# Low halves of the first stage's weights: an accumulating transfer in place of VectorE's subtraction

## The chip, the cores and the metric

The kernel runs on one core of a Trainium2 chip. The metric is the device time of one execution in microseconds, 2017.48 us as the median of three runs of the kernel before (2017.06 to 2017.93). The core has TensorE (PE in the profile, with its weight loads as PEld), VectorE (DVE), ScalarE (ACT), GpSimd (POOL) and SyncE (SP), which issues most of the transfers; each works through a queue of its own in order, and they wait for one another by semaphores. SP's and POOL's transfers run on the core's 16 DMA engines.

## The reference

One layer of an encoder on 16 learned and 1024 given tokens of width 1024, all in float32:

```python
h = rmsnorm(h_res, norm1_w[l])
proj = h @ w_in[l]                       # 1024 x 9248
(q, k, v, z, b_raw, a_raw, sc_b, sc_c, sc_x, gate_a, gate_b) = jnp.split(proj, SPLIT_POINTS, axis=-1)
o_dn = gated_deltanet_bidir(q, k, v, z, b_raw, a_raw, ...)
y_a = o_dn @ w_branch_dn[l]
y_b = (sc_b * depthwise_conv_centred(sc_c * sc_x, sc_conv_w[l])) @ w_branch_sc[l]
merged = jax.nn.sigmoid(gate_a) * y_a + jax.nn.sigmoid(gate_b) * y_b
h_res = h_res + merged @ w_out[l]
gu = rmsnorm(h_res, norm2_w[l]) @ w_gate_up[l]
h_res = h_res + (jax.nn.silu(gu[..., :D_FF]) * gu[..., D_FF:]) @ w_down[l]
```

`gated_deltanet_bidir` runs a short convolution over q, k and v, normalises q and k by head, and does a chunked delta-rule scan forwards and backwards for each of 8 heads of 128 columns. The output is a last RMSNorm without the 16 learned tokens.

## The kernel before

**Products in three parts.** A float32 operand is held as two float32r halves: a high half (a rounded copy) and a low half (what the copy lost). A product is high by high, high by low and low by high, so a weight tile of 128 columns needs `wh` and `wl`, each [128, 8, 128]: 128 partitions, 8 blocks of 128 rows of the weight matrix, 128 columns. A matmul holds one block of `wh` or `wl` stationary and moves a part of `hTh` (high half of the input) or `al` (its low half) past it.

**The first stage** takes about half of the kernel. Its work is cut into 69 units of 128 columns of `w_in`: 24 for q, k and v, 24 for the short convolution's three inputs, 16 gates and 5 of z. A unit has two or three column ranges of tokens, and for each 8 steps of three matmuls (line 321), in the order high-high, high-low, low-high; so the third matmul of a unit's first step needs `wl`. Between the steps the kernel puts the small matmuls of the delta rule's other work, which runs head by head: decays, norms, an inverse of triangular blocks, and the scan (lines 787 to 865), where PE, DVE and ACT hand each other small tiles. The order of everything in this stage is written out by a planner at build time. It keeps a clock for each engine (`T`), adds an estimate for each instruction (`V(n)` for DVE, `A(n)` for ACT, `pe(ns)`), and takes up a piece of the head's work at the step where its clocks say that the inputs are there.

**Weights of a unit.** At the start of unit n, `pick` has SP load the raw weights of unit n+2 (line 917, 512 KB into one of two `raw` slots), and `wtiles` takes the tiles `wh` and `wl` for unit n+1 (two buffers each). `split_part` then makes the halves of unit n+1 in four parts of four blocks each, at the steps given by `SPL`, here 11 to 14 of unit n: ACT copies to `wh` (line 927), DVE writes `wl` as raw minus `wh` (line 924), twice in turn. The first two units' low halves are made by POOL at the start (line 1052), and the third's before the loop by `split_part`.

**POOL** has little else: clearing of row buffers (370, 371, 410), of `small`, `fP`, `mP`, `XT`, a small product (555), and for each head a chain of 30 tiny operations (646, 648) on a 16 x 16 block.

**Later stages** load their weights with the same column blocks of 128 (`wload` for the branches, `stationary1` for the feed-forward part), always through SP, and split them with ACT and DVE (lines 86 and 87).

Of the kernel before, what the change touches and what calls it, by code (L numbers as in the profile page):

```python
# [16 lines left out]
P = 128  # L17
# [16 lines left out]
    0, 1024, 2048, 3072, 4096, 4128, 5152, 6176, 7200, 8224)  # L34


@with_exitstack
def encoder_layer(ctx: ExitStack, tc: tile.TileContext, x, meta, norm1_w, w_in,
                  dn_conv_w, A_log, dt_bias, dn_norm_w, sc_conv_w, w_bdn, w_bsc,
                  w_out, norm2_w, w_gu, w_down, final_w, out):  # L40
    nc = tc.nc
    x, out = x[0], out[0]
    w_in, w_bdn, w_bsc, w_out, w_gu, w_down = (
        w_in[0], w_bdn[0], w_bsc[0], w_out[0], w_gu[0], w_down[0])

    keep = ctx.enter_context(tc.tile_pool(name="keep", bufs=1))
    keep.tile([P, 24], F32, name="pad")
# [37 lines left out]
    def split(hi, lo, src):  # L85
        nc.scalar.copy(hi, src)  # L86
        nc.vector.tensor_tensor(out=lo, in0=src, in1=hi.bitcast(F32), op=ALU.subtract)  # L87
# [11 lines left out]
    def staged(shape):  # L99
        return *wtiles(shape), rawtile(shape)  # L100

    def wload(src, c0, n=P):
        wh, wl, raw = staged([P, KT, P])
        nc.sync.dma_start(raw[:, :, :n], src[:, c0:c0 + n].rearrange("(k p) c -> p k c", p=P))
        split(wh[:, :, :n], wl[:, :, :n], raw[:, :, :n])
        return wh, wl

    def wrows(src, r0):
# [798 lines left out]
    def pick():  # L907

        mid = fill_units and fill_units[0][3] in (1, 2)
        if qkv_units and not mid and qkv_ok():  # L910
            u = qkv_units.pop(0)
        elif fill_units:
            u = fill_units.pop(0)
        else:
            return None
        raw = rawtile([P, KT, P])
        nc.sync.dma_start(raw, w_in[:, u[0]:u[0] + P].rearrange("(k p) c -> p k c", p=P))
        return [u, None, raw, [0]]

    def split_part(u, i):  # L920
        u[3][0] = i + 1
# [48 lines left out]
    with tc.tile_pool(name="st", bufs=1) as st:  # L970
# [18 lines left out]
        for t, xr in enumerate(xs):  # L989
            if t == 0:  # L990
                nc.sync.dma_start(xr[:META], meta)
                nc.sync.dma_start(xr[META:P], x[0:P - META])
                nc.sync.dma_start(w1one, norm1_w[0:1, :])
            else:
                nc.sync.dma_start(xr[:size(t)], x[P * t - META:P * t - META + size(t)])
            if t == 2:
                units.append(pick())

                nc.sync.dma_start(rows[:120, 0], dn_conv_w[0].rearrange("k (t p) -> (k t) p", p=P))
                nc.sync.dma_start(rows[:24, 1], sc_conv_w[0].rearrange("k (t p) -> (k t) p", p=P))  # L1000
                nc.sync.dma_start(rows[24:25, 1], dn_norm_w)
                nc.sync.dma_start(raw, w_in[:, OBA:OBA + 32].rearrange("(k p) c -> p k c", p=P))
            elif t == 5:
                units.append(pick())
        u0, u1 = units
# [296 lines left out]
                yield T["act"]  # L1302

    dn = ph1.enter_context(tc.tile_pool(name="dn", bufs=1))
    SPL = (11, 12, 13, 14)
    for g in (gen0, gen1):
        for _ in g:
            pass
# [1 line left out]
    while done < H or qkv_units or fill_units or any(ahead):  # L1310
        u = ahead.pop(0)
        if u is None:
            run_streams()
            pump()
            T["pe"] += 100
            ahead.append(pick())
            continue
        for k in range(u[3][0], 4):
            split_part(u, k)
        if ahead[0]:  # L1320
            ahead[0][1] = wtiles([P, KT, P])
        ahead.append(pick())
        for n_, _ in enumerate(u[0][1](u[1])):
            if ahead[0] and n_ in SPL:
                split_part(ahead[0], SPL.index(n_))
            run_streams()
            pump()
    ph1.close()
# [14 lines left out]
    mg = [big("mA", [P, 4, SEQ], F32), big("mB", [P, 4, SEQ], F32)]  # L1343
    szs = {}
    for h in range(ZH, H):
        w = wload(w_in, OZ + h * P)
        sz = szs[h] = mg[1][:, h - ZH]
        for i in range(2):
            po = psany()
            dense(po, w, hx, C0 + META + 512 * i, 512)  # L1350
            sl = slice(512 * i, 512 * i + 512)
            nc.scalar.activation(sz[:, sl], po, AF.Tanh, scale=0.5)
            nc.vector.scalar_tensor_tensor(out=sz[:, sl], in0=sz[:, sl], scalar=1.0, in1=po, op0=ALU.add, op1=ALU.mult)
# [19 lines left out]

    gated_order = [*range(ZH, H), *range(ZH)]
    for j in range(KT):
        w = wload(w_bsc, j * P)
        if j == 0:
            for h in range(ZH, H):
                gated(gated_order.pop(0))
# [8 lines left out]
            gated(gated_order.pop(0))  # L1388
    woh, wol = four("w")
    for j in range(KT):  # L1390
        w = wload(w_bdn, j * P)
        ta = s4(SEQ)
        nc.sync.dma_start(ta, ta_d[j])
        for i in range(2):
# [63 lines left out]
    def stationary1(j):  # L1458

        gh, gl = wtiles([P, KT, P])  # L1460
        rg = rawtile([P, KT, P])
        spare.extend(rawtile([P, KT, P]) for _ in range(0 if j else 2))
        ru = rawtile([P, KT, P])
        nc.sync.dma_start(rg, w_gu[:, j * P:j * P + P].rearrange("(k p) c -> p k c", p=P))
        nc.sync.dma_start(ru, w_gu[:, FF + j * P:FF + j * P + P].rearrange("(k p) c -> p k c", p=P))
        if j:
            split(gh, gl, rg)
        return rg, ru, {"A11": (gh[:, 0:4], gl[:, 0:4]), "A12": (gh[:, 4:8], gl[:, 4:8])}, (gh, gl)
# [234 lines left out]
    for n, (a, b, bank) in enumerate((("A11", "B11", bank_x), ("A12", "B21", bank_y), ("S2", "T2", bank_x), ("S1", "T1", bank_y),  # L1703
# [30 lines left out]
                finish(4 + t)  # L1734


_INS = ["x", "meta_tokens", "norm1_w", "w_in", "dn_conv_w", "A_log", "dt_bias", "dn_norm_w", "sc_conv_w",
        "w_branch_dn", "w_branch_sc", "w_out", "norm2_w", "w_gate_up", "w_down", "final_norm_w"]


# [17 lines left out]
```

## Time and profile before

| | |
|---|---|
| median of three runs | 2017.48 us |
| the profiled execution | 2017.61 us |
| its span, first to last instruction | 2015.9 us |
| PE busy | 1994.2 us (99%) |
| DVE busy | 1359.8 us (67%) |
| ACT busy | 819.4 us (41%) |
| POOL busy | 119.6 us (6%) |
| share of PE in the chain that ended last | 88% |

The first stage lasts from the start to about 1045 us of the span. Busy time of PE counts a matmul from its start to its modelled end; since matmuls overlap, 99% doesn't mean that each starts as soon as it could. A wait is given as `engine tile line <- engine tile line`: who sat idle, and whose end released it. In a timeline the columns are start, duration, engine, line, operation, output and inputs, count, and in brackets the idle time before it with what ended it.

### The profile page before, as it was taken

The page shows a single profiled execution, that of the slowest core. Times are in us where ns is not written, and L with a number is a line of the kernel's source. Part 1 is how long each engine was busy: PE and PEld are TensorE (multiplying, and loading weights), DVE is VectorE, ACT ScalarE, POOL GpSimd, SP SyncE. Part 2 cuts the span into 40 slices and gives each one's busy share as a digit, 9 for nine tenths or more (in the row PEclk, how much of TensorE's full clock was granted, in tenths as well). Part 3 has the DMA queues.
Part 4 walks back from the last instruction along what each step waited for, and adds up shares of the span by engine and source line. Part 5 has one row for each costly group of instructions (what it writes and reads, how often), then busy time and mean ns, then how long its engine had stood idle before and what let it go on. Part 6 is the DMA issues. An engine that isn't in the chain of part 4 may idle for free.

```text
span 2015.9 us, 32058 instructions
## 1 busy us (share of the span) xinstructions
PE 1994.2 (99%) x12115; PEld 1735.1 (86%) x12115; DVE 1359.8 (67%) x2982; ACT 819.4 (41%) x1939; POOL 119.6 (6%) x407
## 2 busy tenths in 40 slices
PE   9999999999999999999999999998999999999998
PEld 8999999999999988888888888887888888878887
DVE  6889586888888776866245444459867567646575
ACT  6462345454555464633334121224333333334344
POOL 2002200101020202020000000000000000000000
PEclk9999999999999999999999999999999999999999
DMA  4132322222223232233237643123775245477654
GB/s 133 44 89 63 75 79 69 74 48 74 59 54 95 58 100 64 85 100 90 63 102 243 204 146 95 63 84 112 264 244 205 95 157 180 160 268 248 194 173 167
DMA packets 250579, 247.87 MB, mean 123 GB/s; under 512 B 46070, under 2 KB 190759, under 8 KB 247992
## 3 DMA queue, kind: packets, MB, share of 16 engines
q1 hardware_dynamic: 249847, 244.77, 39.2%
q8 instruction: 95, 1.56, 0.3%
q10 hardware_dynamic: 576, 1.05, 0.1%
q14 instruction: 61, 0.49, 0.1%
HBM read 179.10 MB, written 66.67 MB: 122 GB/s over the span
## 4 chain that ended last, share of the span: by engine, by line
PE 88%; DVE 7%; ACT 2%; DMA 1%; issue 1%; SPq 0%; POOL 0%; ACTq 0%; DVEq 0%; POOLq 0%
PE pm L321 33%; PE pe L1496 7%; PE pd L1496 7%; PE pm L1496 5%; PE pd L802 1%; PE pe L120 1%; PE pe L119 1%; PE pe L121 1%; PE pd L822 1%; PE pd L120 1%; PE pd L119 1%; PE pd L121 1%; PE pe L1670 1%; PE pe L1672 1%; PE pd L819 1%; PE pe L1671 1%
## 5 line engine op out<-in xcount | busy, mean ns | idle before, releaser
L321 PE MATMUL pm<-hTh,wh 128*128 128x512 f32 (+4 forms) x1424 | 518.2, 369 | 0.9 <-ACT kq L373 0.5
L321 PE MATMUL pm<-hTh,wl 128*128 128x512 f32 (+4 forms) x1424 | 483.4, 344 | 0.0
L321 PE MATMUL pm<-al,wh 128*128 128x512 f32 (+4 forms) x1424 | 482.6, 343 | 0.0
L321 PEld LDWEIGHTS pm<-hTh,wh 128*128 128x128 f32 x1424 | 267.0, 188 | 20.4 <-issue 1.7
L321 PEld LDWEIGHTS pm<-hTh,wl 128*128 128x128 f32 x1424 | 266.2, 188 | 19.9 <-DVE wl L924 0.3
L321 PEld LDWEIGHTS pm<-al,wh 128*128 128x128 f32 x1424 | 267.4, 189 | 14.4
L87 DVE TENSOR_TENSOR al<-raw,ring_h 128x1024 fp32r<-128x1024 f32 x73 | 88.7, 1223 | 69.3 <-ACT ring_h L86 68.5
L924 DVE TENSOR_TENSOR wl<-raw,wh 128x512 fp32r<-128x512 f32 x134 | 90.7, 687 | 50.6 <-ACT wh L927 50.0
L86 ACT CAST ring_h<-raw 128x1024 fp32r<-128x1024 f32 x73 | 76.6, 1053 | 107.3 <-PE pe L1672 35.0
L343 DVE SCALAR_TENSOR_TENSOR kq<-ra,wc,kq 128x520 f32<-128x520 f32 x128 | 96.6, 754 | 3.4 <-ACT kq L373 1.9
L927 ACT CAST wh<-raw 128x512 fp32r<-128x512 f32 x134 | 79.1, 621 | 13.3 <-PE pm L321 9.6
L86 ACT CAST wh<-raw 128x1024 fp32r<-128x1024 f32 x43 | 45.1, 1049 | 90.1 <-PE pe L120 32.6
L476 DVE TENSOR_TENSOR tm<-fP,fN 128x135 f32<-128x135 f32 (+23 forms) x248 | 71.5, 288 | 5.0 <-DMA fN<-nd 0.6
L809 ACT ACTIVATE w<-pd,small 128x128 f32<-128x128 f32 x128 | 40.1, 365 | 84.9 <-PE pd L802 77.6
L480 DVE TENSOR_TENSOR fP<-fP,tm 128x135 f32<-128x135 f32 (+23 forms) x248 | 71.2, 287 | 4.9
L831 DVE SCALAR_TENSOR_TENSOR S<-S,eGl,pd 128x128 f32<-128x128 f32 x104 | 31.9, 344 | 51.0 <-PE pd L819 32.7
L87 DVE TENSOR_TENSOR wl<-raw,wh 128x1024 fp32r<-128x1024 f32 x43 | 52.4, 1219 | 11.6 <-ACT wh L86 11.5
L1605 ACT ACTIVATE b<-b 128x512 f32<-128x512 f32 x22 | 13.9, 631 | 107.5 <-DVE b L1498 107.5
L646 POOL TENSOR_TENSOR tm<-mP,mN 1x15 f32<-1x15 f32 (+7 forms) x120 | 42.5, 355 | 220.9 <-DMA mN<-ndm 212.4
L343 DVE SCALAR_TENSOR_TENSOR vT<-ra,wc,vT 128x520 f32<-128x520 f32 x64 | 48.3, 755 | 3.6 <-ACT vT L373 2.6
L514 ACT ACTIVATE PQ<-PQ,negG 128x128 f32<-128x128 f32 x128 | 43.2, 394 | 14.6 <-DVE PQ L509 14.5
L859 ACT ACTIVATE jk<-NP 128x128 f32<-128x128 f32 x64 | 19.8, 310 | 71.8 <-DVE NP L855 70.9
(547 smaller groups left out, 4439.3 us busy)
## 6 DMA issues: line engine op xcount, KB each, us to landing
raw<-in_w_in_dram SPq DMA_DIRECT2D x72, 512.0 KB
raw<-in_w_gate_up_dram SPq DMA_DIRECT2D x44, 512.0 KB
sums<-in_w_down_dram SPq DMA_DIRECT2D x22, 512.0 KB
t_d<-sums SPq DMA_DIRECT2D x11, 1024.0 KB
raw<-s_d SPq DMA_DIRECT2D x44, 256.0 KB
raw<-t_d SPq DMA_DIRECT2D x44, 256.0 KB
act_d<-b SPq DMA_DIRECT2D x43, 256.0 KB
raw<-act_d SPq DMA_DIRECT2D x33, 256.0 KB
```

The source lines that it names most:

```text
L86: nc.scalar.copy(hi, src)
L87: nc.vector.tensor_tensor(out=lo, in0=src, in1=hi.bitcast(F32), op=ALU.subtract)
L119: mm(po[:m, :n], wh[:, k, :m], xhk[:, t0:t0 + n], start=(k == 0), stop=False)
L321: mm(po[:, :n], ww[:, k], f(k)[:, t0:t0 + n], start=i == 0, stop=i == 3 * KT - 1)
L343: nc.vector.scalar_tensor_tensor(out=acc, in0=raw[:, h0 + t:h0 + t + hn], scalar=wc[:, t, col:col + 1], in1=acc, op0=ALU.mult, op1=ALU.add)
L476: nc.vector.tensor_tensor(out=tv, in0=fP[:, 0:r, j:j + 1].broadcast_to([P, r, n]), in1=fN[:, j:j + 1, j + 1:32].broadcast_to([P, r, n]), o ...
L480: nc.vector.tensor_tensor(out=fP[:, 0:r, j + 1:32], in0=fP[:, 0:r, j + 1:32], in1=tv, op=ALU.subtract)
L514: nc.scalar.activation(PQ[:, c, d], PQ[:, c, d], AF.Exp, bias=negG2[:, c, hd:hd + 1])
L646: nc.gpsimd.tensor_tensor(out=tv, in0=mP[:, 0:j + 1, j:j + 1].broadcast_to([1, j + 1, n]), in1=mN[:, j:j + 1, j + 1:META].broadcast_to([1, ...
L924: nc.vector.tensor_tensor(out=u[1][1][:, k], in0=u[2][:, k], in1=u[1][0][:, k].bitcast(F32), op=ALU.subtract)
L927: nc.scalar.copy(u[1][0][:, k], u[2][:, k])
L1496: mm(po, x[:, k], y, start=k + i == 0 and not add_to, stop=k == 3 and i == 2, skip_group_check=add_to)
```

## The change

The low halves of units 4 to 69 of the first stage are no longer made by DVE. At steps 2 and 4 of the unit before, ACT copies four blocks to `wh`; at steps 3 and 5 ACT writes the negated `wh` into `wl`; at step 8 POOL issues a transfer that adds the raw weights, read again from DRAM, onto `wl`. The planner's bookkeeping for the four parts moves with them: four times `A(512)`, where two were `V(512)`. The load of the raw weights by SP stays, since the copy to `wh` reads them.

The host also lays out `w_in`, `w_branch_dn`, `w_branch_sc` and `w_gate_up` by units: 128 columns of all 8 blocks become one array [128, 8, 128] that lies in DRAM as it will lie in SBUF. A partition's part of a unit is then one row of 4 KB, where it was 8 pieces of 512 bytes. The 32 columns for beta and decay are a tensor of their own, `w_ba`.

```diff
+def unit(col):
+    return (col if col < OBA else col - 32) // P
+
+def units(w):
+    return w.reshape(KT, P, -1, P).transpose(2, 1, 0, 3)
...
-    def wload(src, c0, n=P):
+    def wload(src, j):
         wh, wl, raw = staged([P, KT, P])
-        nc.sync.dma_start(raw[:, :, :n], src[:, c0:c0 + n].rearrange("(k p) c -> p k c", p=P))
-        split(wh[:, :, :n], wl[:, :, :n], raw[:, :, :n])
+        nc.sync.dma_start(raw, src[j])
+        split(wh, wl, raw)
         return wh, wl
...
         raw = rawtile([P, KT, P])
-        nc.sync.dma_start(raw, w_in[:, u[0]:u[0] + P].rearrange("(k p) c -> p k c", p=P))
+        nc.sync.dma_start(raw, w_in[unit(u[0])])
         return [u, None, raw, [0]]
+
+    def low_part(u, i):
+
+        k = slice(4 * (i // 2), 4 * (i // 2) + 4)
+        if i == 4:
+            nc.gpsimd.dma_start(u[1][1], w_in[unit(u[0][0])], accum_op=ALU.add)
+        elif i % 2:
+            nc.scalar.activation(u[1][1][:, k], u[1][0][:, k].bitcast(F32), AF.Copy, scale=-1.0)
+            A(512)
+        else:
+            nc.scalar.copy(u[1][0][:, k], u[2][:, k])
+            A(512)
...
-                nc.sync.dma_start(raw, w_in[:, OBA:OBA + 32].rearrange("(k p) c -> p k c", p=P))
+                nc.sync.dma_start(raw, w_ba)
...
-    SPL = (11, 12, 13, 14)
+    SPL = (2, 3, 4, 5, 8)
...
         for n_, _ in enumerate(u[0][1](u[1])):
             if ahead[0] and n_ in SPL:
-                split_part(ahead[0], SPL.index(n_))
+                low_part(ahead[0], SPL.index(n_))
+                ahead[0][3][0] = 4
             run_streams()
             pump()
...
-        nc.sync.dma_start(rg, w_gu[:, j * P:j * P + P].rearrange("(k p) c -> p k c", p=P))
-        nc.sync.dma_start(ru, w_gu[:, FF + j * P:FF + j * P + P].rearrange("(k p) c -> p k c", p=P))
+        nc.sync.dma_start(rg, w_gu[j])
+        nc.sync.dma_start(ru, w_gu[NF + j])
```

What that does to the queues of DVE, ACT and POOL can be seen at three places. Lines of the changed kernel up to about 900 stand 9 lower, so its L806 is L797 of before. First DVE in the first head's scan, around the operations `r0` (L797) that the scan's next matmuls wait for. Before:

```order
L855 TENSOR_TENSOR NP_171_1501<-pd_465_3317,NP_171_1501 128x128
L924 TENSOR_TENSOR wl_450_3256<-raw_389_3002,wh_449_3255 128x512
L797 SCALAR_TENSOR_TENSOR r0_482_3401<-pd_480_3395,negEG_733,vS_334_2753 128x128
L797 SCALAR_TENSOR_TENSOR r0_483_3403<-pd_480_3395,negEG_733,vS_334_2753 128x128
L476 TENSOR_TENSOR tm_484_3405<-fP_339_2761,fN_338_2760 128x112
```

The same place after the change:

```order
L864 TENSOR_TENSOR NP_164_1462<-pd_459_3271,NP_164_1462 128x128
L806 SCALAR_TENSOR_TENSOR r0_477_3356<-pd_475_3350,negEG_733,vS_328_2683 128x128
L806 SCALAR_TENSOR_TENSOR r0_478_3358<-pd_475_3350,negEG_733,vS_328_2683 128x128
L485 TENSOR_TENSOR tm_479_3360<-fP_333_2691,fN_332_2690 128x112
L352 SCALAR_TENSOR_TENSOR vT_147_1326<-ra_451_3229,wc_146,vT_147_1326 128x520
```

The subtraction into `wl` stood ahead of the two `r0`, and nothing stands there now. Next ACT, at the same place before, with the copies to `wh` on either side of the scan's squares (L859), and ahead of the scan's `w` (L809):

```order
L927 CAST wh_449_3255<-raw_389_3002 128x512
L859 ACTIVATE jk_478_3378,small_131_1285<-NP_171_1501 128x128
L859 ACTIVATE jk_479_3382,small_131_1285<-NP_171_1501 128x128
L927 CAST wh_449_3255<-raw_389_3002 128x512
L809 ACTIVATE w_488_3426<-pd_480_3395,small_131_1285 128x128
L809 ACTIVATE w_489_3428<-pd_480_3395,small_131_1285 128x128
```

and after, some steps of the same scan earlier, where one unit's four parts now stand together:

```order
L938 CAST wh_386_2958<-raw_342_2752 128x512
L935 ACTIVATE wl_387_2959<-wh_386_2958 128x512
L938 CAST wh_386_2958<-raw_342_2752 128x512
L935 ACTIVATE wl_387_2959<-wh_386_2958 128x512
L818 ACTIVATE w_403_3034<-pd_396_3000,small_125_1244 128x128
L818 ACTIVATE w_404_3036<-pd_396_3000,small_125_1244 128x128
```

ACT has twice as many parts of a unit to do, ahead of the `w` that the scan's matmuls wait for. Last POOL, within the chain of tiny operations of the second head, before:

```order
L646 TENSOR_TENSOR tm_411_3092<-mP_341_2763,mN_340_2762 1x60
L648 TENSOR_TENSOR mP_341_2763<-mP_341_2763,tm_411_3092 1x10x6
L646 TENSOR_TENSOR tm_417_3113<-mP_341_2763,mN_340_2762 1x55
L648 TENSOR_TENSOR mP_341_2763<-mP_341_2763,tm_417_3113 1x11x5
```

and after:

```order
L655 TENSOR_TENSOR tm_408_3048<-mP_335_2693,mN_334_2692 1x60
L657 TENSOR_TENSOR mP_335_2693<-mP_335_2693,tm_408_3048 1x10x6
L933 DMA wl_387_2959<-in_w_in_dram 128x1024
L655 TENSOR_TENSOR tm_411_3066<-mP_335_2693,mN_334_2692 1x55
L657 TENSOR_TENSOR mP_335_2693<-mP_335_2693,tm_411_3066 1x11x5
```

The issue of the accumulating transfer stands in POOL's queue behind whatever the chain has to do.

More of the change, by code (lines that the diff above doesn't have):

```diff
@@ L34, with encoder_layer @@
     0, 1024, 2048, 3072, 4096, 4128, 5152, 6176, 7200, 8224)
+def unit(col):
+    return (col if col < OBA else col - 32) // P
+def units(w):
+    return w.reshape(KT, P, -1, P).transpose(2, 1, 0, 3)
 @with_exitstack
-def encoder_layer(ctx: ExitStack, tc: tile.TileContext, x, meta, norm1_w, w_in,
+def encoder_layer(ctx: ExitStack, tc: tile.TileContext, x, meta, norm1_w, w_in, w_ba,
                   dn_conv_w, A_log, dt_bias, dn_norm_w, sc_conv_w, w_bdn, w_bsc,
@@ L42, in encoder_layer @@
     x, out = x[0], out[0]
-    w_in, w_bdn, w_bsc, w_out, w_gu, w_down = (
-        w_in[0], w_bdn[0], w_bsc[0], w_out[0], w_gu[0], w_down[0])
+    w_out, w_down = w_out[0], w_down[0]
     keep = ctx.enter_context(tc.tile_pool(name="keep", bufs=1))
@@ L1345, in encoder_layer @@
     for h in range(ZH, H):
-        w = wload(w_in, OZ + h * P)
+        w = wload(w_in, unit(OZ + h * P))
         sz = szs[h] = mg[1][:, h - ZH]
@@ L1375, in encoder_layer @@
     for j in range(KT):
-        w = wload(w_bsc, j * P)
+        w = wload(w_bsc, j)
         if j == 0:
@@ L1390, in encoder_layer @@
     for j in range(KT):
-        w = wload(w_bdn, j * P)
+        w = wload(w_bdn, j)
         ta = s4(SEQ)
@@ L1734, in encoder_layer @@
                 finish(4 + t)
-_INS = ["x", "meta_tokens", "norm1_w", "w_in", "dn_conv_w", "A_log", "dt_bias", "dn_norm_w", "sc_conv_w",
+_INS = ["x", "meta_tokens", "norm1_w", "w_in", "w_ba", "dn_conv_w", "A_log", "dt_bias", "dn_norm_w", "sc_conv_w",
         "w_branch_dn", "w_branch_sc", "w_out", "norm2_w", "w_gate_up", "w_down", "final_norm_w"]
@@ L1748 @@
     arrays, args = {}, []
+    laid = {k: _np.asarray(inputs[k]) for k in _INS if k in inputs}
+    w = laid["w_in"][0]
+    laid["w_in"] = units(_np.concatenate([w[:, :OBA], w[:, OBA + 32:]], axis=1))
+    laid["w_ba"] = w[:, OBA:OBA + 32].reshape(KT, P, 32).transpose(1, 0, 2)
+    for k in ("w_branch_dn", "w_branch_sc", "w_gate_up"):
+        laid[k] = units(laid[k][0])
     for name in _INS:
-        a = _np.ascontiguousarray(inputs[name])
+        a = _np.ascontiguousarray(laid[name])
         arrays[f"in_{name}_dram"] = a
```

## The prediction

> **What bounds the kernel now.** I read the busy times first, then the chain that ended last, the first stage and one later stretch as windows, and last what PE and its weight loads waited for in the first stage (60 to 1010 us, the last row from 0 to 1062; columns: total, times, longest).
>
> ```profile
> PE 1994.2 (99%) x12115; PEld 1735.1 (86%) x12115; DVE 1359.8 (67%) x2982; ACT 819.4 (41%) x1939; POOL 119.6 (6%) x407
> PE 88%; DVE 7%; ACT 2%; DMA 1%; issue 1%; SPq 0%; POOL 0%; ACTq 0%; DVEq 0%; POOLq 0%
> 60.00:1010.00 950.00, 945.72 (x7312) 863.49 (x7311) 714.20 (x2004) 447.02 (x1400) 107.63 (x371) 1.00 0.27 73
> 1100.00:1150.00 50.00, 50.00 (x223) 41.38 (x222) 25.23 (x27) 11.27 (x11) 0.00 (x0) 1.00 0.69 227
> ...
> PE pd L802 <- DVE r L797: 3.4, 6, 0.8
> ...
> PEld pd L802 <- DVE r L797: 5.8, 9, 1.2
> PEld pd L819 <- ACT v L814: 2.2, 10, 0.5
> PEld pd L769 <- ACT vS L761: 1.6, 5, 0.4
> ...
> PEld pm L321 <- DVE wl L924: 0.3, 1, 0.3
> ```
>
> TensorE bounds it everywhere, at a granted clock of 1.00, and the number of its matmuls isn't touched. So the change can move only the few microseconds in which PE stands still: some 4 us of 950 by the matmul rows, more by the weight loads, since a matmul's modelled end covers a part. Two things are to be seen. The weights themselves are never late (0.3 us, once), so making them sooner is worth nothing. What PE waits for most is `r0` of the scan (L797) on DVE, and that is where the removed subtractions may count. No transfer of weights stands among PE's waits, so the new layout, as such, is costed at nothing: what hides it is the load one and a half units ahead.
>
> **Removed: the subtractions on DVE.** The longest waits for `r0`, in time, as PE saw them (start, duration, engine, line):
>
> ```profile
> 281.36 0.35 PE L321 MATMUL pm<-al,wh 128*128 128x384 f32 x1
> 281.54 0.34 PE L321 MATMUL pm<-hTh,wl 128*128 128x384 f32 x1
> 282.61 0.38 PE L802 MATMUL pd<-r,NP 128*128 128x128 f32 x1 [0.73 <-DVE r L797]
> ...
> 368.95 0.31 PE L321 MATMUL pm<-hTh,wl 128*128 128x336 f32 x1
> 369.49 0.38 PE L802 MATMUL pd<-r,NP 128*128 128x128 f32 x1 [0.22 <-DVE r L797]
> ...
> 381.39 0.33 PE L321 MATMUL pm<-hTh,wl 128*128 128x384 f32 x1
> 382.58 0.38 PE L802 MATMUL pd<-r,NP 128*128 128x128 f32 x1 [0.85 <-DVE r L797]
> ...
> 710.77 0.33 PE L321 MATMUL pm<-hTh,wl 128*128 128x384 f32 x1
> 711.96 0.38 PE L802 MATMUL pd<-r,NP 128*128 128x128 f32 x1 [0.85 <-DVE r L797]
> ```
>
> A matmul of 384 columns is followed after 0.18 us (281.36 to 281.54). The four pauses from start to start are 1.07, 0.54, 1.19 and 1.19 us, so PE lost 0.89, 0.36, 1.01 and 1.01 us: 3.3 us. What stood before `r0` on DVE, and before that on ACT:
>
> ```profile
> 280.40 0.31 ACT L859 ACTIVATE jk<-NP 128x128 f32<-128x128 f32 x1 [0.18 <-DVE NP L855]
> 280.71 0.60 ACT L927 CAST wh<-raw 128x512 fp32r<-128x512 f32 x1
> ...
> 280.02 0.29 DVE L855 TENSOR_TENSOR NP<-pd,NP 128x128 f32<-128x128 f32 x1
> 281.35 0.69 DVE L924 TENSOR_TENSOR wl<-raw,wh 128x512 fp32r<-128x512 f32 x1 [1.04 <-ACT wh L927]
> 281.96 0.60 DVE L797 SCALAR_TENSOR_TENSOR r<-pd,negEG,vS 128x128 f32<-128x128 f32 x2
> ...
> 368.22 0.69 DVE L924 TENSOR_TENSOR wl<-raw,wh 128x512 fp32r<-128x512 f32 x1 [1.04 <-ACT wh L927]
> ...
> 381.31 0.69 DVE L924 TENSOR_TENSOR wl<-raw,wh 128x512 fp32r<-128x512 f32 x1 [1.04 <-ACT wh L927]
> ...
> 710.69 0.69 DVE L924 TENSOR_TENSOR wl<-raw,wh 128x512 fp32r<-128x512 f32 x1 [1.04 <-ACT wh L927]
> ```
>
> All four are one pattern: ACT's squares (L859) wait for DVE, the copy to `wh` stands behind them, DVE's subtraction waits 1.04 us for the copy, and `r0` stands behind the subtraction: 1.04 + 0.6 us of delay that the scan doesn't need. The change takes the subtraction out of DVE's queue, and in the rows of the order nothing takes its place ahead of `r0`. **First term: -3.3 us.**
>
> ```profile
> L924 DVE TENSOR_TENSOR wl<-raw,wh 128x512 fp32r<-128x512 f32 x126 | 85.4, 688 | 45.1 <-ACT wh L927 44.5
> L927 ACT CAST wh<-raw 128x512 fp32r<-128x512 f32 x126 | 74.4, 621 | 9.7 <-PE pm L321 9.6
> L1605 ACT ACTIVATE b<-b x22: 622/632/633, 1405.4 to 1795.8; 128x512 f32<-128x512 f32 x22
> ```
>
> DVE loses 85.4 us of work and 44.5 us of standing behind ACT: 130 of 950 us. Of the 5.8 us that weight loads waited for `r0` about 4 are the four places; I let the other 1.8 shrink by a third. **Second term: -0.6 us** (bounds 0 and -1.8).
>
> **Added: the negated copies on ACT.** 66 units with two each are 132 activations. The nearest row of that size from SBUF to SBUF takes 632 ns, the copy to `wh` 621: 132 x 0.63 = 83 us, which takes ACT in this stage from 447 to 530 us of 950. ACT has room; the price is delay of what stands behind. Up to four parts in a row are 2.5 us ahead of the scan's `w` (L809), which PE's L819 waits for. PE's waits that ACT ends are 2.2 + 1.6 us above; if they grow as ACT's work does (83/447 = 19%), **third term: +0.7 us**. Bounds: 0, since a fuller clock of the planner also moves the scan's matmuls behind other steps; and +3.3, if ACT's parts meet the scan as often as DVE's did.
>
> **Added: the accumulating transfer.** No row of this kernel holds one, or any load issued by POOL. It reads 512 KB from DRAM and 512 KB from `wl`, and writes 512 KB. The nearest rows are one plain load, and a transfer of 1024 KB that shares the engines with a load (issue by SP; then windows whose last two columns are the busy share of the 16 DMA engines and GB/s):
>
> ```profile
> 347.71 0.39 SPq L917 DMA_DIRECT2D raw<-in_w_in_dram  x1
> ...
> 347.70:351.50 3.80, 3.80 (x27) 3.79 (x27) 0.58 (x4) 1.14 (x4) 1.37 (x6) 1.00 0.74 211
> 351.50:353.00 1.50, 1.50 (x11) 1.37 (x10) 0.88 (x4) 0.74 (x2) 1.11 (x5) 1.00 0.00 0
> ...
> 824.18 0.34 SPq L505 DMA_DIRECT2D PQ<-grow  x1
> 824.63 0.37 SPq L917 DMA_DIRECT2D raw<-in_w_in_dram  x1
> ...
> 824.10:830.10 6.00, 6.00 (x35) 5.74 (x34) 5.10 (x22) 2.52 (x8) 0.00 (x0) 1.00 0.80 263
> 830.10:832.00 1.90, 1.90 (x10) 1.54 (x9) 1.90 (x10) 0.00 (x0) 0.00 (x0) 1.00 0.04 6
> ```
>
> One load is done at most 3.8 us after its issue, 1.5 MB at most 5.9 us. I take 5 us, nearer to the second because the bytes moved are more alike. If reading and adding can't overlap at all, twice the load is 7.6 us.
>
> [...]
>
> How long may it take? It is issued at step 8, and the next unit's first step needs `wl`. The shortest units have two ranges of 512 columns, 16 steps; by the window above a matmul of 512 columns takes 50/223 = 0.224 us, so 8 steps x 3 are 5.4 us at least. With the scan's work between them a half of such a unit takes longer:
>
> ```profile
> L440 ACT ACTIVATE rb<-pm x13: 577/598/617, 902.1 to 993.9; 128x512 f32<-128x512 f32 x13
> ```
>
> 91.8 us for 12 halves is 7.65 us. Units with three ranges (950 us / 63 = 15.1 us each on average, two thirds left at step 8) leave about 10 us. So 29 units (16 gates, 8 of the short convolution, 5 of z) have between 5.4 and some 9.9 us, the others more, and a transfer of 5 us is always in time. Spread evenly, lateness at t us sums to 29 x (t - 5.4)^2 / 9: 0.8 us at 5.9, and 8 us at 7. **Fourth term: +0.2 us.**
>
> Behind POOL's queue stands the issue itself. POOL is busy 108 of 950 us; its tiny operations (30 in a chain) cost the issue a fraction of a us each, and what the issue delays in turn, the chain, is covered by DVE's 62 operations for the same head:
>
> ```profile
> L646 POOL TENSOR_TENSOR tm<-mP,mN 1x15 f32<-1x15 f32 (+7 forms) x120 | 42.5, 355 | 220.9 <-DMA mN<-ndm 212.4
> L476 DVE TENSOR_TENSOR tm<-fP,fN 128x135 f32<-128x135 f32 (+23 forms) x248 | 71.5, 288 | 5.0 <-DMA fN<-nd 0.6
> ```
>
> 62 x 0.288 = 18 us against 30 x 0.36 = 11 us. **Sum:** -3.3 - 0.6 + 0.7 + 0.2 = -3.0 us. The span of 2015.9 becomes 2012.9; the profiled execution, 2017.6 with 1.7 us around its span, agrees with the median of 2017.5, so I predict 2014.5 us. That is 0.15%; a change of under 0.2% (4.0 us) can't be told from none here.
>
> **The rivals.** *A clear gain*: DVE's relief goes further than the four places and ACT costs nothing, -3.3 - 1.8 = -5.1 us, 2012.4. For it: DVE is busy or held 759 of 950 us before and 629 after, and much of what PE awaits is at the end of DVE's chain. Against: ACT feeds the same scan.
>
> *The transfer is late*: it takes 7.5 us, and the first step of two-range units waits. 29 x 2.1^2 / 9 = 14 us lost, 11 net: 2029. It decides from t = 6.4 us, where 29 x 1 / 9 = 3.2 us eats the gain. For it: no row shows how fast POOL issues or the engines add. Against: both loads above stay under 6 us. [...]
>
> *ACT takes DVE's place*: the four parts stand ahead of `w` as the subtraction stood ahead of `r0`, and all 3.3 us come back: 2017.5 - 0.6 + 0.2 = 2017.1, within 0.2%.
>
> **How the numbers follow.** My forecast and ACT's return (both within 0.2%) together 0.42; the clear gain 0.34; the late transfer, with smaller mishaps of the same sign, 0.24. Likeliest is no change that can be told, with its own range 2013.5 to 2018. The range for 8 in 10 reaches from 2010.5, somewhat beyond the clear gain, to 2029, the late transfer at 7.5 us; slower than that I give 0.08.
>
> **What would show it.** In the changed profile the four pauses before L811 (L802 before) are gone; PE's waits for `r0` fall from 5.8 us to about 1.5; DVE's busy time in the stage falls by 85 us and ACT's rises by 83; PE never waits for the accumulating transfer; the later stages keep their times. I am wrong if weight loads of L330 wait for a transfer into `wl`, if waits on ACT's `w` or `v` grow by more than 2 us, or if a stage after 1050 us changes.

## The result, and the profile after

The changed kernel takes 2032.8 us (median; 2031.8 to 2034.0), the kernel before 2017.7 on the same chip (2017.1 to 2018.1): a ratio of 1.0077, 95% interval 1.0065 to 1.0090. It is slower by 15 us. The forecast was 2014.5, the range ended at 2029.0, and 2032.8 lies outside it.

All of the loss is in the first stage. Two rows of the view of one source line, the first of the kernel before, the second of the changed one (line 321 became 330; the last two numbers are the starts of the line's first and last instruction):

```profile
L321 PEld LDWEIGHTS pm<-hTh,wh x1424: 186/188/192, 17.2 to 1060.2; 128*128 128x128 f32 x178
```

```profile
L330 PEld LDWEIGHTS pm<-hTh,wh x1424: 186/188/338, 16.6 to 1075.9; 128*128 128x128 f32 x178
```

The stage ends 15.7 us later. (So before the change it lasts to about 1060 us of the span, not to 1045 as said above.) From there to the end of the span it is 2030.7 - 1075.9 = 954.8 us, against 2015.9 - 1060.2 = 955.7 before.

The page of the changed kernel, busy times and the chain that ended last:

```profile
PE 2000.3 (99%) x12115; PEld 1738.4 (86%) x12115; DVE 1285.6 (63%) x2850; ACT 895.9 (44%) x2071; POOL 163.7 (8%) x473
...
PE 84%; DVE 7%; DMA 5%; ACT 2%; issue 1%; SPq 1%; DVEq 0%; ACTq 0%; POOL 0%
```

DVE lost 74 us of work and ACT gained 77; 85 and 83 were foretold. But DMA rose from 1% to 5% of the chain. What that is, the waits of the changed kernel in the first 1080 us show (engine, line, what it waited for: total us, times, longest):

```profile
DVE XT L686 <- DMA NP<-pd: 27.1, 7, 7.3
...
ACT Xe L682 <- DMA NP<-pd: 23.2, 6, 7.7
...
PEld pm L330 <- DMA wl<-in_w_in_dram: 7.4, 5, 3.9
...
PEld pd L702 <- DVE Xe L688: 3.3, 3, 2.1
...
PEld pd L811 <- DVE r L806: 2.8, 7, 0.8
...
PEld pd L702 <- DVE XT L686: 1.5, 1, 1.5
```

The same view of the kernel before, over the same stretch:

```profile
ACT Xe L673 <- DMA NP<-pd: 18.6, 4, 6.3
...
DVE XT L677 <- DMA NP<-pd: 7.2, 5, 3.0
...
PEld pd L802 <- DVE r L797: 6.2, 10, 1.2
```

Three things have changed. The wait for `r0` (L802, now L811) has fallen from 6.2 to 2.8 us, as forecast. PE now waits for the accumulating transfer into `wl` (7.4 us; there was no such row). And PE waits in the inverse (L702) for `Xe` and `XT`, since DVE and ACT themselves stand longer for `NP<-pd`: the second half of a round trip in which the inverse's blocks are written to DRAM (`pd<-fP`) and read back in another layout. One such trip before, then the same one after, in the view of the timeline (start, duration, engine, line):

```profile
736.27 1.67 SPq L656 DMA_DIRECT2D pd<-fP  x3
...
744.69 1.92 SPq L661 DMA_DIRECT2D NP<-pd  x4
...
746.75 0.43 DVE L677 STREAM_TRANSPOSE XT<-NP 32x256 f32<-32x256 f32 x1 [3.03 <-DMA NP<-pd]
```

```profile
735.40 2.07 SPq L665 DMA_DIRECT2D pd<-fP  x3
...
742.28 0.88 POOL L933 DMA_DIRECT2D wl<-in_w_in_dram  x1 [7.93 <-ACT wl L935]
...
744.74 2.33 SPq L670 DMA_DIRECT2D NP<-pd  x4
...
749.99 0.43 DVE L686 STREAM_TRANSPOSE XT<-NP 32x256 f32<-32x256 f32 x1 [7.31 <-DMA NP<-pd]
750.20 0.40 ACT L682 COPY Xe<-NP 32x256 f32<-32x256 f32 x1 [7.69 <-DMA NP<-pd]
...
750.48 0.24 PE L702 MATMUL pd<-XT,NP 32*32 32x32 f32 x2 [1.10 <-DVE XT L686]
```

An accumulating transfer was issued 2.5 us before `NP<-pd`, and from the issue of `NP<-pd` to the transposition it is 5.2 us in place of 2.1. DVE, with everything in its queue, stands for 7.3 us in place of 3.0, ACT for 7.7, and PE runs into the inverse's first products before they have their operands. Over the eight heads, from the issue of `pd<-fP` to the first transposition, it is 11.1 us on average before and 13.2 after; the longest 12.0 and 15.4. (In the head with 15.4 the transposition didn't wait for the transfer. In the changed order without the accumulating transfers, a run below, the average is 11.6, so the transfers themselves add 1.6 us.) The planner allows 5.5 + 5.6 = 11.1 us for it (`LAND`, and the 5600 ns behind the second issue): there was no slack.

### The profile page after: what moved, and what is told of

Same layout as the page of the kernel before. It is cut to its first block, busy times and chain, and to the rows that moved or that the text cites. A ratio compares the mean times of both kernels' runs of the same rounds, so it can differ in the third digit from the quotient of the medians.

```text
span 2030.7 us, 32187 instructions
## 1 busy us (share of the span) xinstructions
PE 2000.3 (99%) x12115; PEld 1738.4 (86%) x12115; DVE 1285.6 (63%) x2850; ACT 895.9 (44%) x2071; POOL 163.7 (8%) x473
## 3 DMA queue, kind: packets, MB, share of 16 engines
q0 software_dynamic: 9504, 34.61, 10.3%
## 4 chain that ended last, share of the span: by engine, by line
PE 84%; DVE 7%; DMA 5%; ACT 2%; issue 1%; SPq 1%; DVEq 0%; ACTq 0%; POOL 0%
PE pm L330 30%; PE pd L1518 7%; PE pe L1518 7%; PE pm L1518 5%; DMA pd<-fP 2%; PE pd L811 1%; PE pe L129 1%; PE pe L130 1%; PE pe L128 1%; PE pd L828 1%; DMA wl<-in_w_in_dram 1%; PE pe L580 1%; PE pd L831 1%; PE pd L129 1%; PE pd L130 1%; PE pd L128 1%
## 5 line engine op out<-in xcount | busy, mean ns | idle before, releaser
L330 PE MATMUL pm<-hTh,wh 128*128 128x384 f32 (+4 forms) x1424 | 519.7, 370 | 1.5 <-ACT ra L423 0.7
L330 PE MATMUL pm<-hTh,wl 128*128 128x384 f32 (+4 forms) x1424 | 484.3, 345 | 5.8 <-DMA wl<-in_w_in_dram 5.8
L330 PE MATMUL pm<-al,wh 128*128 128x384 f32 (+4 forms) x1424 | 482.9, 344 | 0.0
L330 PEld LDWEIGHTS pm<-hTh,wl 128*128 128x128 f32 x1424 | 266.5, 188 | 27.1 <-DMA wl<-in_w_in_dram 7.4
L933 POOL DMA_DIRECT2D wl<-in_w_in_dram x66 | 57.9, 877 | 699.9 <-ACT wl L935 534.7
L935 ACT ACTIVATE wl<-wh 128x512 fp32r<-128x512 f32 x132 | 83.3, 631 | 3.1
L381 ACT COPY ra<-pm 128x336 f32<-128x336 f32 (+2 forms) x72 | 32.0, 445 | 40.8 <-PE pm L330 40.7
L806 DVE SCALAR_TENSOR_TENSOR r<-pd,negEG,vS 128x128 f32<-128x128 f32 x120 | 36.7, 345 | 20.4 <-PE pd L796 19.6
```

The source lines that it names most:

```text
L330: mm(po[:, :n], ww[:, k], f(k)[:, t0:t0 + n], start=i == 0, stop=i == 3 * KT - 1)
L933: nc.gpsimd.dma_start(u[1][1], w_in[unit(u[0][0])], accum_op=ALU.add)
L935: nc.scalar.activation(u[1][1][:, k], u[1][0][:, k].bitcast(F32), AF.Copy, scale=-1.0)
```

## The experiments

Theory T says that the loss comes from the traffic of the accumulating transfers. Its rivals are A (ACT's added work and the earlier steps), P (POOL's queue), and later G, H and L; C is a narrower form of T. All times are medians; ratios are to the kernel before, timed in turn with each run. The kernel before took 2016.6 to 2017.8 us beside the different runs, so a difference of a microsecond between two runs goes by their ratios.

### One part at a time

**The layout alone.** From the changed kernel, the old split is put back:

```diff
-    SPL = (2, 3, 4, 5, 8)
+    SPL = (11, 12, 13, 14)
-                low_part(ahead[0], SPL.index(n_))
-                ahead[0][3][0] = 4
+                split_part(ahead[0], SPL.index(n_))
```

> The layout alone: weights in units of 128 columns, but the low parts as before, by DVE's subtraction at steps 11 to 14, and no accumulating transfer. Theory T (traffic): the loss of the change comes with the accumulating transfers, which share the DMA engines with the inverse's trips through DRAM (pd<-fP, NP<-pd) and with each other; so the layout alone gives 2017 us, within 2 us of before, and DVE's XT waits about 7 us in total for NP<-pd, as before (27 with the change). Theory A (ACT): the loss comes from ACT's 132 negations and the earlier steps; it expects 2017 too. If the layout alone is slower by more than 4 us, both fall.

Measured: 2016.5 us, ratio 0.9995 (0.9986 to 1.0004). The layout costs and brings nothing that can be told.

**The change without its transfer.**

```diff
-            nc.gpsimd.dma_start(u[1][1], w_in[unit(u[0][0])], accum_op=ALU.add)
+            pass
```

> The change without its accumulating transfer: the negated copies stand as low parts (this leaves the low parts of the first stage's weights out of the result), all engines' instructions stay in the same order. Theory T: the waits for wl (7 us) and the later NP<-pd go, and TensorE's clock stays at 1.00 after 750 and 900 us; with the four pauses before r0 gone the time is 2013 to 2016 us. Theory A: ACT's negations are still there, so the time stays at 2027 to 2033 us, less only what waits for wl took.

Measured: 2013.5 us, ratio 0.9983 (0.9974 to 0.9991). Theory A falls: with all of ACT's 132 negations and the same order the kernel is faster than before. One issued instruction a unit makes 19 us (span 2030.7 against 2011.7). Its waits for `r0` and for the trips:

```profile
DVE XT L686 <- DMA NP<-pd: 16.5, 7, 4.5
...
ACT Xe L682 <- DMA NP<-pd: 11.8, 6, 4.7
...
PEld pd L811 <- DVE r L806: 2.8, 7, 0.8
```

No row of L702 waiting for `Xe` or `XT` is left, and no half clock in the first stage (the longest weight load of line 330 into `pm<-hTh,wh` takes 192 ns, where the changed kernel has 338).

**The transfer, with no reader.** The same bytes are added onto the tile `raw`, which is dead by then:

```diff
-            nc.gpsimd.dma_start(u[1][1], w_in[unit(u[0][0])], accum_op=ALU.add)
+            nc.gpsimd.dma_start(u[2], w_in[unit(u[0][0])], accum_op=ALU.add)
```

> The change with the same accumulating transfer, of the same size and at the same step, but added onto the raw tile, which nobody reads any more at that point, so that no matmul waits for its landing (this leaves the low parts out of the result). Theory T in its first form (traffic slows the inverse's trips): the waits of DVE and ACT for NP<-pd stay (about 35 us of DVE's), L702's waits stay at about 5 us, and only the 7 us of waits for wl and what the clock loses behind them go: 2022 to 2026 us. If the late weights are everything: 2013 to 2017 us. Theory A: 2022 to 2026 too, so this run speaks for T only beside the one without a transfer.

Measured: 2024.5 us, ratio 1.0038 (1.0025 to 1.0051). So 11 of the 19 us are lost although nobody waits for the transfer; the other 8 are lost only when PE waits for it, and belong to late weights and what follows them. The inverse's waits are all there:

```profile
DVE XT L686 <- DMA NP<-pd: 29.9, 7, 7.3
...
ACT Xe L682 <- DMA NP<-pd: 28.4, 7, 7.5
...
PEld pd L702 <- DVE Xe L688: 3.4, 4, 1.8
```

**The earlier steps alone**, with DVE's subtraction at steps 2 to 5 and no transfer:

```diff
-    SPL = (2, 3, 4, 5, 8)
+    SPL = (2, 3, 4, 5)
-                low_part(ahead[0], SPL.index(n_))
-                ahead[0][3][0] = 4
+                split_part(ahead[0], SPL.index(n_))
```

> The layout and the earlier steps alone: the split at steps 2 to 5 in place of 11 to 14, but by DVE's subtraction, with no negation on ACT and no transfer. Theory T: the steps cost little; 2015 to 2020 us, DVE standing behind ACT's copies as before. If the earlier steps are what costs (the copies stand ahead of the conv rows and the scan on ACT at the start of a unit): above 2022 us.

Measured: 2022.7 us, ratio 1.0027 (1.0017 to 1.0037); the second expectation came true, though not its reason, since ACT's copies stand at the same steps in the run without a transfer (2013.5). Splitting early costs some 6 us as long as DVE does the subtraction, and nothing once ACT negates instead; the planner's order differs between the two as well. Which of PE's products carries it was not settled.

### What of the transfer it is

**An eighth of the bytes**, one row of eight, same issue, same place in POOL's queue:

```diff
+            nc.gpsimd.dma_start(u[2][:, 0:1], w_in[unit(u[0][0])][:, 0:1], accum_op=ALU.add)
```

> As the run with the transfer onto the raw tile, but only one of its eight rows (64 KB in place of 512 KB); POOL issues it at the same step and stands in its queue behind the same copies on ACT (the low parts are left out of the result as there). Theory T (traffic): an eighth of the bytes, so the time is near that without a transfer, 2013.5 to 2016 us, and XT comes 11.0 to 11.8 us after pd<-fP on average. [...]

Measured: 2014.7 us, ratio 0.9991 (0.9982 to 1.0000). XT comes 11.8 us after `pd<-fP` on average, as theory T expected. Theory P, by which the loss lies in POOL's queue and the time would have stayed at 2022 to 2026 us, falls: POOL's waiting and its issuing (872 ns each here too) cost one or two microseconds at most.

**A plain load of the same bytes by POOL**, nothing added:

```diff
+            nc.gpsimd.dma_start(u[2], w_in[unit(u[0][0])])
```

> As the run with the transfer onto the raw tile, but a plain load of the same 512 KB by POOL, which overwrites and adds nothing (low parts left out as there). Theory T by all bytes moved: a plain load moves two thirds of what an accumulating one does (read, write; no second read), and it is shorter on the engines, so about half of the 11 us remain: 2017 to 2021 us. If only the adding is slow (a transfer that holds the engines longer): 2013.5 to 2016. If any load of POOL's costs the same, or theory P: 2022 to 2026.

Measured: 2016.5 us, ratio 1.0002 (0.9993 to 1.0010), 3 to 4 us over no transfer, against 11 for the accumulating one. That lies between two expectations, just above the one by which only the adding is slow and just below theory T by all bytes. DVE's wait for `NP<-pd` (L686) orders the runs in the same way: 16.5 us without a transfer, 23.0 with the plain load, 29.9 with the accumulating one onto `raw`. The software queue's row in the page's third part (packets, MB, time of the packets as a share of the 16 engines' span), first with accumulation, as in the changed kernel, then with the plain load:

```profile
q0 software_dynamic: 9504, 34.61, 10.3%
```

```profile
q0 software_dynamic: 9504, 34.61, 5.4%
```

For the same packets and bytes the accumulating form holds the DMA engines almost twice as long: 0.103 x 2030.7 / 66 = 3.2 us of all 16 engines for each transfer, against 0.054 x 2014.3 / 66 = 1.65 us.

**Only some of the transfers.** In the trace of the changed kernel, 12 of the 66 transfers were under way between the issue of `pd<-fP` and the first transposition. Theory C says that these collisions do the harm, theory G that every transfer costs alike. Both runs keep the order of all other instructions:

```diff
+            sent.append(u)
+            if len(sent) - 1 not in (10, 11, 17, 23, 24, 31, 32, 38, 44, 45, 50, 56):
+                nc.gpsimd.dma_start(u[1][1], w_in[unit(u[0][0])], accum_op=ALU.add)
```

> The change, in the same order, without the 12 of its 66 accumulating transfers that in its trace were under way between the issue of pd<-fP and XT, so that 54 stay (the low parts of those 12 units are left out of the result). Theory C (collisions with the inverse's return trips cost, and what is held behind them): 2014 to 2018 us, almost as without any transfer. Theory G (every transfer costs the same, 19.3/66 us): 2032.8 - 12 x 0.29 = 2029 us, 2028 to 2031.

Measured: 2014.9 us, ratio 0.9984 (0.9975 to 0.9993), with 54 transfers left. The complement has `in` in place of `not in`:

> The complement: only these 12 transfers, the other 54 left out (and their low parts). Theory C: most of the 19 us is lost with 12 transfers alone, 2027 to 2033 us. Theory G: 2013.5 + 12 x 0.29 = 2017 us, 2016 to 2019.

Measured: 2029.2 us, ratio 1.0054 (1.0041 to 1.0066), with 12 transfers. Theory G falls by both. First the waits with 54 transfers, then with the 12:

```profile
DVE XT L686 <- DMA NP<-pd: 16.7, 7, 4.6
...
ACT Xe L682 <- DMA NP<-pd: 11.5, 5, 4.8
...
PEld pm L330 <- DMA wl<-in_w_in_dram: 0.4, 1, 0.4
```

```profile
DVE XT L686 <- DMA NP<-pd: 31.8, 7, 7.4
...
ACT Xe L682 <- DMA NP<-pd: 27.2, 7, 7.9
...
PEld pd L702 <- DVE Xe L688: 3.5, 4, 1.5
...
PEld pm L330 <- DMA wl<-in_w_in_dram: 3.0, 3, 1.6
PEld pd L702 <- DVE XT L686: 2.9, 2, 1.6
```

The harm goes both ways in a collision: the trip lands late, and so does the transfer into `wl` (weight loads wait 3.0 us for the 12). Without the 12 the other 54 weights are never late by more than 0.4 us. Since the order is the same with and without transfers, PE's matmuls of line 330 can be compared one by one: of the 19.0 us by which the changed kernel falls behind the run without a transfer, 18.7 arise at 300 to 320, 380 to 390, 400 to 420, 520 to 530, 630 to 650, 750 to 760 and 940 to 950 us. All of these but the second (1.3 us) stand at or behind one of the inverse's trips.

### Covering the wait

**An earlier transfer**, all steps moved forward:

```diff
-    SPL = (2, 3, 4, 5, 8)
+    SPL = (1, 2, 3, 4, 5)
```

> The change with all its steps earlier (1 to 4 for ACT's copies and negations, 5 for the transfer in place of 8), arrival times of the inverse as in the change. Theory L (the weights are late because the transfer is issued too late for its 5.6 to 10.3 us): about 2 us earlier takes away most of the 7 us of waits for wl, and the time is that with the transfer onto the raw tile, 2022 to 2027 us. Theory H (held engines: the weights are late only because ACT, held for NP<-pd, negates late): three steps don't help, 2029 to 2035 us.

Measured: 2034.6 us, ratio 1.0085 (1.0071 to 1.0099). The waits for `wl` are 6.5 us where they were 7.4, so theory L falls as stated. Theory H named the right number, but the trace does not bear out its reason: the three that held PE longest were issued right behind their negations and landed 7 to 9.6 us later. Two of them were issued at the start of or within one of the inverse's trips, the third 0.4 us behind a load of 1 MB (`PQ<-grow`).

**Later planned arrivals**, 2 us on each half of the trip:

```diff
-    LAND = 5500
+    LAND = 7500
-        yield T["pe"] + 5600
+        yield T["pe"] + 7600
```

> The change, with the planner expecting each of the inverse's transfers through DRAM 2 us later (7.5 and 7.6 us in place of 5.5 and 5.6), so that DVE and ACT come to the transposes and copies of NP after it has landed. Theory T: DVE's and ACT's waits for NP<-pd fall from about 62 us together to under 20, L702's waits to under 1 us, and the time by 5 to 9 us, to 2024 to 2028; the waits for wl stay. If the held engines are off the path: 2031 to 2034. If the inverse itself becomes late by its longer planned trips (8 us a head), waits of the scan on it appear and the time rises above 2034.

Measured: 2011.3 us (2010.8 to 2011.9), ratio 0.9974 (0.9963 to 0.9984): 21 us faster than the change, and 5 faster than the kernel before, with the whole computation. It gained more than any theory gave it. The late weights went as well, and no stretch of half clock is left in the first stage (the longest weight load of line 330 takes 193 ns):

```profile
ACT Xe L682 <- DMA NP<-pd: 12.2, 3, 7.7
...
DVE XT L686 <- DMA NP<-pd: 5.9, 2, 5.6
...
PEld pm L330 <- DMA wl<-in_w_in_dram: 0.5, 1, 0.5
```

**The same arrivals without the change** (layout alone, old split):

> The layout alone with the later arrivals (7.5 and 7.6 us in place of 5.5 and 5.6): DVE's subtraction at steps 11 to 14, no transfer. This tells what the later arrivals are worth without the change. If they only mend what the transfers delay: 2015 to 2018 us, like the layout alone (2016.5). If DVE and ACT were held in the kernel before too (7 and 19 us for NP<-pd) and PE paid for it: 2011 to 2014 us, and then the 2011.3 us of the change with later arrivals is mostly not the change's.

Measured: 2018.9 us, ratio 1.0008 (0.9999 to 1.0017), a little above the first expectation. In this order the later arrivals bring nothing. **And without the transfer** (change, later arrivals, transfer left out):

> The change without its transfer (low parts left out of the result) and with the later arrivals. Against the change with later arrivals (2011.3 us) it tells what the transfers still cost once nobody waits in order for the inverse's trips. Theory T with the wait as the only path: 2010 to 2011.5 us, the transfers cost under 1 us. If traffic costs in another way too: 2005 to 2009 us.

Measured: 2010.4 us, ratio 0.9965 (0.9953 to 0.9978): with these arrivals all 66 transfers together cost 1 us by the medians and 2 by the ratios, in place of 19. Of the 21 us some 3 are due to the order itself, since without a transfer the later arrivals bring 2013.5 down to 2010.4.

**Other arrival times**, 1 us and 4 us later:

> The change with arrivals planned 1 us later in place of 2 (6.5 and 6.6 us). Theory C: trips that take 13.2 us on average (10.7 to 15.4) from pd<-fP to XT, where 11.1 were planned and now 13.1, are covered in about half the heads: 2016 to 2024 us, between the change and 2011. A lucky order at 2 us alone: 2028 us or more.

Measured: 2024.4 us, ratio 1.0030 (1.0018 to 1.0041).

> The change with arrivals planned 4 us later (9.5 and 9.6 us): 19.1 us planned for trips that take at most 15.4. Theory C: nothing more to cover beyond 2 us, so 2010 to 2014 us, as long as the inverse, 16 us later in each head, isn't late for the scan. If it is, waits of PE for what the inverse makes appear and the time is above 2016. A lucky order at 2 us alone: 2020 us or more.

Measured: 2014.3 us, ratio 0.9982 (0.9973 to 0.9991). Both lie just above the upper end of what theory C allowed, and a lucky order at 2 us alone (2028 or more, 2020 or more) falls. Three rows of the run with 1 us tell more:

```profile
DVE XT L686 <- DMA NP<-pd: 43.6, 7, 14.9
...
PEld pm L330 <- DMA wl<-in_w_in_dram: 8.4, 6, 2.3
...
PEld pd L702 <- DVE Xe L688: 0.4, 1, 0.4
```

The inverse's products no longer wait, although DVE stands longer for `NP<-pd` (43.6 us) than in the change (27.1): what costs is a product of the inverse that comes late, not the standing as such. The weights still wait. So these are two losses, and the later arrival mends only the first for certain. The waits for the weights (8.4 us) don't cover the 13 us by which this run is slower than the one with 2 us; the rest was not laid out. The last run on this puts both edits together, arrivals 2 us later and the transfer at step 5:

> The change with arrivals planned 2 us later and all its steps earlier (transfer at step 5 in place of 8). Theory C with the trips covered: what is left is the landing of the weights, and three steps more for it leave no waits for wl; 2009 to 2013 us. If late weights depend on which transfers the one into wl meets, and so on the order, waits for wl of 3 to 8 us can appear again: 2014 to 2022 us, and the 2011.3 us would be partly the luck of one order.

Measured: 2018.0 us, ratio 1.0003 (0.9994 to 1.0012), with the late weights back:

```profile
PEld pm L330 <- DMA wl<-in_w_in_dram: 6.9, 3, 2.7
```

The second expectation of this run came true, and part of the 2011.3 us is the luck of one order. All three late transfers were issued within a trip of the inverse, between `pd<-fP` and `NP<-pd`, and landed 8.3 to 10.0 us later. In the run of 2011.3 us eight transfers were issued within a trip as well, the slowest landed after 8.4 us, and yet no weight was late by more than 0.5 us. So a late weight takes more than a meeting with a trip; that it also depends on how soon the unit is needed is likely, but was not tested.

### Without a transfer, for comparison

**ACT's copies further ahead of DVE's subtractions**, with the layout and the old arrivals:

```diff
-    SPL = (11, 12, 13, 14)
+    SPL = (8, 12, 10, 14)
```

> The layout, no transfer, arrivals as before, DVE's subtractions at steps 12 and 14, ACT's copies two steps or more ahead at 8 and 10. The four pauses before r0 were priced at 3.3 us: if they come from DVE standing behind ACT's copy, this version takes 2012 to 2014 us, against 2016.5 of the layout with the copies one step ahead. With later arrivals the same edit gained 5.7 us. If the gain needed the later arrivals: 2016 to 2018.

Measured: 2015.9 us, ratio 0.9992 (0.9983 to 1.0001). The wait for `r0` falls from 6.2 to 1.0 us. The time, against 2016.5 with the copies one step ahead, falls by no more than can be told; that is close to the second expectation:

```profile
PEld pd L828 <- ACT v L823: 4.5, 20, 0.5
...
PEld pd L811 <- DVE r L806: 1.0, 3, 0.5
```

PE's pauses before `r0` were real, but taking them away shifted the plan, and part came back elsewhere: the wait for ACT's `v` rose to 4.5 us from 2.2 in the layout alone. Where the rest went was not settled. **With the later arrivals besides:**

> A version without a transfer and with the whole result: layout, later arrivals, DVE's subtractions at steps 12 and 14, but ACT's copies two steps or more ahead of them, at 8 and 10, so that DVE doesn't stand behind a copy. If the four pauses before r0 come from that standing (3.3 us before the change), it gains 2 to 4 us on the layout with later arrivals. If any subtraction of DVE ahead of r0 costs, it gains under 1 us.

Measured: 2013.2 us, ratio 0.9979 (0.9970 to 0.9988), 5.7 us below the layout with those arrivals, where 2 to 4 were expected. It is faster than before without any accumulating transfer.

**The subtraction on POOL**, in place of negation and transfer:

```diff
-            nc.scalar.activation(u[1][1][:, k], u[1][0][:, k].bitcast(F32), AF.Copy, scale=-1.0)
-            A(512)
+            nc.gpsimd.tensor_tensor(out=u[1][1][:, k], in0=u[2][:, k], in1=u[1][0][:, k].bitcast(F32), op=ALU.subtract)
```

> The low parts by a subtraction on POOL in place of ACT's negation and the transfer, in the new layout, at steps 3 and 5 (copies of ACT at 2 and 4); the result is complete. POOL's rows for such a subtraction in the prologue take 1.29 us, so 132 of them are 170 us of POOL's 950. Theory T: no transfer, so no loss from it; ACT has 83 us less than in the run without a transfer, so 2012 to 2015 us, faster than before. Against it: if POOL and DVE slow each other down on SBUF, or POOL's chain for the inverse comes late behind the subtractions, 2018 us or more.

Measured: 2046.7 us, ratio 1.0147 (1.0133 to 1.0161): the expectation against it came true, and by far more than its mark. Two of DVE's groups over the first 1060 us, first in the run without a transfer, then here:

```profile
L485 DVE TENSOR_TENSOR tm<-fP,fN 128x135 f32<-128x135 f32 (+23 forms) x248 | 71.4, 288 | 5.2
...
L603 DVE SCALAR_TENSOR_TENSOR NP<-pe,small,PQ 128x128 f32<-128x128 f32 x128 | 38.5, 341 | 5.2 <-PE pe L580 3.1 <-ACT PQ L523 1.9
```

```profile
L485 DVE TENSOR_TENSOR tm<-fP,fN 128x135 f32<-128x135 f32 (+23 forms) x248 | 88.7, 358 | 5.1 <-DMA fN<-nd 0.2
...
L603 DVE SCALAR_TENSOR_TENSOR NP<-pe,small,PQ 128x128 f32<-128x128 f32 x128 | 38.4, 340 | 3.4 <-PE pe L580 3.1
```

These DVE operations with both operands in SBUF take 24% longer (288 to 358 ns), and other such groups of 128 x 512 or 520 take 7 to 18% longer; those that read one operand from PSUM (`pe`, `pd`) stay within 2%. How much of the 30 us this is, beside POOL's own queue, was not separated.

## Why the prediction was wrong, by its own steps

**What bounds the kernel** held: PE throughout, and the loss appeared as PE standing still. But the sentence that the change can move only the few microseconds in which PE stands still limits a gain and not a loss, and the granted clock did not stay at 1.00 (0.50 and 0.51 in two stretches, below). **The layout at nothing** held (0.9995). **The first two terms** held as a mechanism: the long pauses before `r0` are gone but for one of 0.8 us, and the weight loads' wait for it fell from 6.2 to 2.8 us (to about 1.5 was foretold). **The sum of the first three terms** held: the change without its transfer gained 3.8 us (0.9 to 2.6 thousandths), where they gave 3.2. The single terms are not shown by that, and the agreement may in part be luck, since taking away the waits for `r0` in another way gained 0.6 us. **POOL's queue at nothing** held, within one or two microseconds.

**The fourth term failed: the accumulating transfer at +0.2 us.** It cost 19 us. The typical landing time was not the error. The estimate was 5.0 us, the measured median 5.6:

```profile
L933 POOL DMA_DIRECT2D wl<-in_w_in_dram x66: 858/875/1055, 57.8 to 1058.6; - x66
...
DMA to landing us min/median/max: 5.0/5.6/10.3
```

By the term's own formula 5.6 us would cost 29 x 0.2^2 / 9 = 0.1 us. The term asked one question, whether the transfer is in time for its own reader, as if it were alone. It left out two others. What does it do to transfers already under way? The trace of before held the rows that could have warned: DVE 7.2 and ACT 18.6 us waiting for `NP<-pd`, a trip without slack, in front of engines that work in order. And how long does the slowest one take? The formula spread the units' time evenly and took one landing time for all; the one of 10.3 us held a weight load for 3.9 us. 12 transfers of 66 make most of the loss.

The 19.0 us between the spans with and without the transfer can mostly be laid out: 7.4 us of weight loads waiting for `wl`, 4.8 us of L702 waiting for `Xe` and `XT` (3.3 + 1.5), and, by an estimate, 4.6 us of lower clock behind them (below). The remaining 2.2 us were not laid out.

**The rival of the late transfer** (2029 us) came nearest in number, by another mechanism. It had all transfers at 7.5 us and the first step of the two-range units waiting; in fact half landed within 5.6, five weight loads waited, and 11 us were lost where no one read the transfer's result. **The signs**: "PE never waits for the accumulating transfer" came out wrong, and by the text's own list that was a mark of error. PE's waits for ACT's `v` did not grow (2.2 to 2.0 us), and the later stages kept their time.

The issue on POOL took 858 to 1055 ns throughout. The profile counts 34.61 MB for the transfers with accumulation and for the plain loads alike; what it shows of the adding is the time on the DMA engines, 10.3 against 5.4%. Both loads that the estimate of 5.0 us was taken from were done within 5.9 us; the accumulating transfer was at the median (5.6) and not at its slowest (10.3).

## What to carry to other kernels

A transfer that nothing waits for isn't free (here 11 us, with the transfer onto `raw`): ask which transfer in flight has no slack, which in-order engine stands in front of it, and charge the new traffic there. A planner's fixed landing time belongs to the traffic it was measured in (here a trip of 11.1 us on average became one of 13.2); when traffic is added, that number has to be measured again, and then the change can pay (2032.8 to 2011.3 us by three constants, though 2018.0 in another order). Price a transfer by its slowest landing in company as well as by its median alone.

## What the hardware showed that was not expected

**A short stall can be paid twice.** Busy time and granted clock of the changed kernel by windows (window; length; busy PE, PEld, DVE, ACT, POOL; PE's granted clock; DMA share; GB/s):

```profile
749.30:752.70 3.40, 1.61 (x67) 1.31 (x67) 2.58 (x7) 2.42 (x7) 0.00 (x0) 1.00 0.04 6
752.70:759.50 6.80, 5.78 (x107) 3.92 (x106) 4.00 (x12) 0.95 (x3) 0.00 (x0) 0.50 0.11 41
...
937.00:940.40 3.40, 0.28 (x1) 0.27 (x2) 0.00 (x0) 0.00 (x0) 0.00 (x0) 1.00 0.22 53
940.40:943.80 3.40, 3.40 (x13) 2.92 (x12) 1.31 (x4) 1.21 (x3) 0.00 (x0) 0.51 0.63 123
```

Behind the stalls at 750 and 937 us the clock is halved for 6.8 and 3.4 us (0.50 and 0.51 in the rows above; weight loads of line 330 take up to 0.34 us there, where their median is 0.19), which by an estimate costs 5.78 / 2 + 3.4 / 2 = 4.6 us at the lower clock. Before the change, and without the transfer, the first stage has no such stretch; the longest weight load of that line (321 before) takes 192 ns in both. The other runs with a loss by collisions have them: two of 3.4 us with the transfer onto `raw`, and 3.4, 3.4 and 6.8 us with the 12 transfers alone; the longest weight load takes 337 ns in both, and the granted clock over the whole span is 0.996 and 0.994, against 0.998 before. What halves the clock was not shown. PE was not idle ahead of the first stretch: in the window at 749.30 it was busy for 1.61 of 3.4 us, and its longest gap there was 1.1 us. A busy share alone does not decide it: with arrivals 1 us later PE was busy for 1.66 of 3.4 us, and the clock stayed at 1.00.

```profile
492.70:496.10 3.40, 1.66 (x10) 1.38 (x8) 3.40 (x17) 1.98 (x4) 0.52 (x3) 1.00 0.82 222
496.10:499.50 3.40, 3.33 (x24) 3.31 (x25) 3.26 (x11) 1.63 (x5) 0.00 (x0) 1.00 0.01 2
```

What tells the two apart stays open; the first window held 67 products, most of them of 32 x 32, the second 10.

**POOL and DVE on SBUF.** The slowdown of up to 24% above was expected only as a risk. With the subtraction on POOL, DVE's operations with both operands in SBUF went from 288 to 358 ns, and those with one operand from PSUM from 341 to 340. Why only the first are slowed was not shown.
